# Two sweeps over each weight slab, and the gates' one-hot rows made one pair of slabs ahead, in a two-block transformer kernel on one core

## The chip, the cores and the metric

The kernel runs on one core of a Trainium2 chip. The core has five engines that are programmed apart and meet at semaphores: TensorE (PE, with its weight loads as PEld), VectorE (DVE), ScalarE (ACT), GpSimd (POOL) and SyncE (SP, which here issues DMAs). The metric is the device time of one execution, in microseconds (us), as the median of several runs; lower is better.

## The reference, cut to what matters

Two transformer blocks over 256 tokens of width 1024, batch 1, all in float32. The first has differential attention and stick-breaking attention side by side, cross attention to a memory of 256 tokens, and an MLP with a squared ReLU. The second has latent attention (MLA) and an RWKV7 recurrence side by side, and then a PEER layer that chooses 16 of 16384 experts for each of 8 heads of each token:

```python
def first_block(...):
    u = rms_norm(h, g_mix[l]) @ w_in[l]
    ...
    h = h + y @ w_out[l]
    h = h + cross_attention(rms_norm(h, g_cross[l]), rms_norm(mem, g_mem[l]), w_xq[l], w_xkv[l], w_xo[l])
    a = jnp.square(jax.nn.relu(rms_norm(h, g_mlp[l]) @ w_up[l]))
    h = h + a @ w_down[l]

def second_block(...):
    p = h @ w_in[l]
    y_a = mla_group(p[..., :MLA_COLS], ...)
    y_b = rwkv7_group(p[..., MLA_COLS:], ...)
    x = x + jnp.concatenate([y_a, y_b], axis=-1) @ w_o[l]
    x = x + peer_ffn(rms_norm_2(x, g_ffn[l]), w_pq[l], sub_keys[l], expert_u[l], expert_v[l])

def peer_ffn(...):            # inside, for 128 tokens at a time
    ...                       # top 16 of 128 keys twice, then top 16 of the 256 sums
    gate = jax.nn.softmax(top_s, axis=-1).astype(hb.dtype)
    act = jax.nn.gelu(jnp.einsum('thkd,td->thk', expert_u[idx], hb), approximate=False)
    return jnp.einsum('thk,thkd->td', gate * act, expert_v[idx])
```

## The kernel before

**Products in three parts.** A float32 product is made from three products of a narrower type. Each weight matrix comes in slabs of 128 x 1024 values (512 KB, one DMA on SP's queue, three buffers `raw`). `split` makes the slab's high part `hi` on ACT (line 329, three buffers) and then its low part `lo = raw - hi` on DVE (line 331, two buffers). The activations have such a pair too (`xsh`/`xsl`, `hbh`/`hbl` and others). For each 128-row piece of a slab `mm3` issues three products of 256 columns, one behind the other: hi by high activations (line 338), hi by low (line 339), lo by high (line 340). So the third product of a slab's very first piece already needs `lo`, and every later piece stands behind it, since PE works in the order of its instructions. In the MLP (`wide`) the first two are one product of 512 columns (line 398), and the third is at line 400. `lin_tok` and `Lin2.finish` have loops of their own (lines 476 to 478, and `mm3`).

**Stages.** In the profiled execution they are, roughly: first block's input and attentions up to 60 us, the rest of the first block up to 430, the second block's input, MLA and RWKV up to 700, the PEER layer's expert keys (`eu`, 128 slabs in 64 pairs, `u_pair`) up to 1110, and its values (`ev`, 128 slabs, lines 1774 to 1778) to the end. All 16384 experts are computed densely. Beside the `eu` pairs, DVE first works through `choose()` (the top-16 search), which ends with the halving sums of line 1655; after it come 32 gate groups of 8 tokens (`g_group`). A group makes one-hot rows `hot` and `wt` on DVE, multiplies them on PE (16 small products of line 1696) and puts the gates into `GA`. `GA` holds them next to the GELU of the keys' products.

**The order of the work.** The kernel is written against a scheduler that places the instructions of each engine's queue by their readiness in a simulated timeline and by their priority, which follows the order of the code unless `tc.high_priority` raises it. On the chip each engine then runs its queue in that order and waits at semaphores. So a change in one loop moves instructions that it doesn't name. The one on which this bears most is the RWKV part: a small triangular solve, in two rounds (`p_4977` is the first round's buffer, `p_4991` the second's), of short DVE instructions (lines 1152 to 1167), interleaved on DVE with MLA's key norm (`kg`, line 1370) for PE's scores (line 1375).

Of the kernel before, what the change touches and what calls it, by code (L numbers as in the profile page):

```python
# [20 lines left out]
P = 128  # L21
T = 256
D = 1024
KC = D // P
# [26 lines left out]
HI_BUFS = 3  # L51
LO_BUFS = 2
U_STEPS = 3
ATT_BUFS = 2
LIN_PS = 4
AHEAD_A = 2
# [158 lines left out]
def body(tc, A, out):  # L215
# [3 lines left out]
    with es:  # L219
# [117 lines left out]
        def mm3(ps, lh, ll, rh, rl, start, stop):  # L337
            PE.matmul(ps, lhsT=lh, rhs=rh, start=start, stop=False, skip_group_check=True)  # L338
            PE.matmul(ps, lhsT=lh, rhs=rl, start=False, stop=False, skip_group_check=True)  # L339
            PE.matmul(ps, lhsT=ll, rhs=rh, start=False, stop=stop, skip_group_check=True)  # L340

        def act_split(dst, src, j, scale=None):

            hi, lo = dst
            if scale is None:
                S.activation(hi[:, j], src, AF.Copy)
                V.tensor_tensor(lo[:, j], src, hi.bitcast(F32)[:, j], op=OP.subtract)
            else:
                S.activation(hi[:, j], src, AF.Identity, scale=scale)
                V.scalar_tensor_tensor(lo[:, j], src, scale, hi.bitcast(F32)[:, j], op0=OP.mult, op1=OP.subtract)  # L350
# [36 lines left out]
        def lin_part(ps, x, w, k, nb, c0, c1, first=True, wide=False):  # L387


            if ahead:  # L390
                w_ = ahead.pop(0)
                wh, wl = w_ if isinstance(w_, tuple) else split(w_)
            else:
                wh, wl = slab(w[nb][:, c0 * P:c1 * P], (c1 - c0) * P)
            for c in range(c0, c1):
                o = (c - c0) * P
                if wide:
                    PE.matmul(ps.rearrange("p (a t) -> p a t", a=2), lhsT=wh[:, o:o + P], rhs=x.both[:, c], start=first and c == 0,  # L398
                              stop=False, skip_group_check=True)
                    PE.matmul(ps[:, :T], lhsT=wl[:, o:o + P], rhs=x[0][:, c], start=False, stop=c == k - 1, skip_group_check=True)  # L400
                    continue
                mm3(ps[:, :T], wh[:, o:o + P], wl[:, o:o + P], x[0][:, c], x[1][:, c], first and c == 0, c == k - 1)

        def lin_T(x, w, k, nbs, evac, wide=None):

# [1271 lines left out]
            yield  # L1677


        def g_group(g, done):  # L1680

            hot = gp.tile([P, 2, 8, P], F16, tag="o1", name=nm("hot"), bufs=2)
            wt = gp.tile([P, 8, P], F16, tag="oh", name=nm("wt"), bufs=2)
            rows = lambda a: a.rearrange("p s t (a b) -> p (s t) a b", b=2)
            each = lambda a: a[:, g].rearrange("p s t b -> p (s t) b")[:, :, None].to_broadcast([P, 16, P // 2, 2])
            V.tensor_tensor(rows(hot), io[:, None].rearrange("p m (a b) -> p m a b", b=2).to_broadcast([P, 16, P // 2, 2]),
                            each(pk), op=OP.is_equal)
            parts = (wt, hot[:, 1])
            for s, dst in enumerate(parts):
                V.tensor_tensor(dst.rearrange("p t (a b) -> p t a b", b=2), hot[:, 1].rearrange("p t (a b) -> p t a b", b=2),  # L1690
                                pg[:, g, s, :, None].to_broadcast([P, 8, P // 2, 2]), op=OP.mult)
            ps = [pw(i) for i in range(2)]
            for i in range(8):
                p_, o_ = ps[i // 4], (i % 4) * P
                for s in range(2):
                    PE.matmul(p_[:, o_:o_ + P], lhsT=hot[:, 0, i], rhs=parts[s][:, i], start=i % 4 == 0 and s == 0,  # L1696
                              stop=i % 4 == 3 and s == 1, skip_group_check=True)
            for j in range(2):
                q = slice(8 * g + 4 * j, 8 * g + 4 * j + 4)
                p_ = ps[j].rearrange("p (t i) -> p i t", t=4)  # L1700
                if done:
                    V.scalar_tensor_tensor(GA[:, 0:done, q], p_[:, 0:done], 1 / GS, GA[:, 0:done, q], op0=OP.mult, op1=OP.mult)
                if done < P:
                    S.activation(GA[:, done:, q], p_[:, done:], AF.Copy, scale=1 / GS)

        def u_pair(c, td):

            ps = plin()
            for i in range(2):
                wh, wl = slab(A["eu"][c + i])  # L1710
                for k in range(KC):
                    ks = slice(k * P, k * P + P)
                    mm3(ps[:, i * T:i * T + T], wh[:, ks], wl[:, ks], hb[0][:, k], hb[1][:, k], i == 0 and k == 0,
                        i == 1 and k == KC - 1)
            pv_ = ps.rearrange("p (c t) -> p c t", c=2)
            dst = GA[:, c:c + 2]
            if td < T:
# [6 lines left out]

        steps = choose()
        next(steps)
        ng, first = 0, None
        for c in range(0, P, 2):
            u_pair(c, 8 * ng)
            if first is None:  # L1730
                for _ in range(U_STEPS):
                    if next(steps, mix) is mix:
                        first = c + 2
                        break
            else:
                want = min(32, ((c - first) // 2 + 1) * 32 // ((P - first - U_LAST) // 2))
                while ng < want:
                    g_group(ng, c + 2)
                    ng += 1

        acc = [[pw() for _ in range(2)] for _ in range(2)]
        res_ = [[x0("res", "h", 2 * t + d, F32).rearrange("p a t -> p (a t)") for d in range(2)] for t in range(2)]
# [55 lines left out]
```

## Time and profile before

| What | us |
|---|---|
| median of 3 runs | 1473.48 |
| lowest and highest of them | 1471.85, 1476.6 |
| the profiled execution | 1472.92 |
| its span in the trace | 1471.1 |

The profile is that of the one execution of 1472.92 us. Its trace spans 1471.1 us; the other 1.8 us lie around it. An engine's busy time counts its records, and a PE record is longer than the time PE takes until the next one starts, because matmuls overlap; so for PE the distance between starts says more than the busy share. A wait is printed in square brackets behind the instruction that waited, with the work that released it.

### The profile page before, as it was taken

How to read it: one execution, taken by the hardware profiler on the slowest of the kernel's cores; microseconds unless marked ns; L12 is line 12 of the kernel's file. 1: busy time of each engine (PE TensorE's matmuls, PEld its weight loads, DVE VectorE, ACT ScalarE, POOL GpSimd, SP SyncE). 2: the span in 40 equal slices, each digit the busy share in tenths (PEclk: the TensorE clock that was granted, in tenths of full speed). 3: DMA queues.
4: the chain of work that ended last, by engine and by line, in shares of the span. 5: the costliest groups of instructions: out<-in, count | busy, mean ns of one | idle time of the engine just before them, and what ended most of it. 6: DMA issues, size and time to landing. Idle time of an engine off the chain costs nothing.

```text
span 1471.1 us, 25614 instructions
## 1 busy us (share of the span) xinstructions
PE 1436.3 (98%) x9950; PEld 1296.2 (88%) x9950; DVE 1065.2 (72%) x1901; ACT 768.3 (52%) x1248; POOL 147.6 (10%) x159
## 2 busy tenths in 40 slices
PE   8999999999999979999999999999999999999998
PEld 7888999888888857799999999999998888888887
DVE  7876686886669997588998668788885555555554
ACT  7856655555556445463445454444445445444443
POOL 7400101000215352120000000000000000000000
PEclk9999999999999988999999999999999999999999
DMA  7553445666665411155555555555555655656664
GB/s 221 170 154 118 129 145 150 194 187 189 192 191 158 136 30 38 26 180 161 157 174 170 174 172 159 159 159 163 157 166 179 195 193 194 193 194 193 194 194 149
DMA packets 75914, 237.43 MB, mean 161 GB/s; under 512 B 14608, under 2 KB 17808, under 8 KB 75792
## 3 DMA queue, kind: packets, MB, share of 16 engines
q1 hardware_dynamic: 75792, 235.79, 52.2%
q8 instruction: 78, 1.28, 0.4%
q14 instruction: 44, 0.36, 0.1%
HBM read 233.27 MB, written 2.49 MB: 160 GB/s over the span
## 4 chain that ended last, share of the span: by engine, by line
PE 84%; DVE 9%; DMA 3%; ACT 1%; issue 1%; POOL 0%; SPq 0%; DVEq 0%; ACTq 0%
PE lin L340 13%; PE lin L338 13%; PE lin L339 12%; PE w L1774 8%; PE w L1775 8%; PE w L1778 8%; PE lin L398 7%; PE lin L400 3%; DVE lo L331 3%; PE w L1696 2%; DMA raw<-w_down 1%; DMA raw<-eu 1%; PE lin L476 1%; PE lin L478 1%; PE lin L477 1%
## 5 line engine op out<-in xcount | busy, mean ns | idle before, releaser
L331 DVE TENSOR_TENSOR lo<-raw,hi 128x1024 fp32r<-128x1024 f32 (+1 forms) x432 | 529.7, 1226 | 291.7 <-PE w L1775 92.7
L329 ACT ACTIVATE hi<-raw 128x1024 fp32r<-128x1024 f32 x437 | 458.6, 1050 | 464.7 <-PE lin L339 173.9
L340 PE MATMUL lin<-hbh,lo 128*128 128x256 f32 x1024 | 291.4, 287 | 4.1 <-DVE lo L331 4.1
L338 PE MATMUL lin<-hbh,hi 128*128 128x256 f32 x1024 | 291.7, 286 | 0.0
L339 PE MATMUL lin<-hbl,hi 128*128 128x256 f32 x1024 | 288.6, 283 | 0.0
L340 PEld LDWEIGHTS lin<-hbh,lo 128*128 128x128 f32 x1024 | 195.1, 191 | 6.3 <-DVE lo L331 6.0
L338 PEld LDWEIGHTS lin<-hbh,hi 128*128 128x128 f32 x1024 | 196.2, 192 | 0.3 <-ACT hi L329 0.2
L339 PEld LDWEIGHTS lin<-hbl,hi 128*128 128x128 f32 x1024 | 196.1, 192 | 0.0
L1775 PE MATMUL w<-lo,wh 128*128 128x512 f32 x504 | 155.3, 389 | 0.0
L1778 PE MATMUL w<-hi,wl 128*128 128x512 f32 x504 | 155.1, 389 | 0.0
L1774 PE MATMUL w<-hi,wh 128*128 128x512 f32 x504 | 134.8, 389 | 0.0
L1778 PEld LDWEIGHTS w<-hi,wl 128*128 128x128 f32 x504 | 94.6, 188 | 19.6
L1774 PEld LDWEIGHTS w<-hi,wh 128*128 128x128 f32 x504 | 94.5, 188 | 19.6
L1775 PEld LDWEIGHTS w<-lo,wh 128*128 128x128 f32 x504 | 94.5, 188 | 19.6
L398 PE MATMUL lin<-xs,hi 128*128 128x512 f32 x256 | 90.3, 398 | 0.3 <-ACT hi L329 0.3
L398 PE MATMUL lin<-a,hi 128*128 128x512 f32 x256 | 89.6, 394 | 0.0
L1757 ACT ACTIVATE wh<-GA 128x512 fp32r<-128x512 f32 x64 | 40.5, 634 | 74.0 <-PE w L1775 74.0
L400 PE MATMUL lin<-a,lo 128*128 128x256 f32 x256 | 71.4, 283 | 0.6 <-DVE lo L331 0.6
L400 PE MATMUL lin<-xs,lo 128*128 128x256 f32 x256 | 71.5, 281 | 0.0
L522 POOL TENSOR_TENSOR sqa<-sqa,sq 128x256 f32<-128x256 f32 x37 | 33.6, 909 | 315.0 <-ACT sq L518 301.3
L398 PEld LDWEIGHTS lin<-xs,hi 128*128 128x128 f32 x256 | 47.9, 188 | 12.1 <-ACT hi L329 0.7
L398 PEld LDWEIGHTS lin<-a,hi 128*128 128x128 f32 x256 | 47.6, 188 | 10.3
(566 smaller groups left out, 2868.8 us busy)
## 6 DMA issues: line engine op xcount, KB each, us to landing
raw<-eu SPq DMA_DIRECT2D x128, 512.0 KB, 3.6
raw<-ev SPq DMA_DIRECT2D x128, 512.0 KB, 3.5
raw<-w_up SPq DMA_DIRECT2D x32, 512.0 KB, 3.6
raw<-w_down SPq DMA_DIRECT2D x32, 512.0 KB, 4.7
raw<-w_in SPq DMA_DIRECT2D x20, 512.0 KB, 3.8
raw<-w_in_s SPq DMA_DIRECT2D x16, 512.0 KB, 3.6
raw<-w_pq SPq DMA_DIRECT2D x16, 512.0 KB, 3.7
raw<-w_in_m SPq DMA_DIRECT2D x8, 512.0 KB, 3.6
```

Source lines behind the costliest of these rows:

```text
L329: S.activation(hi[:, :n], raw[:, :n], AF.Copy)
L331: eng.tensor_tensor(lo[:, :n], raw[:, :n], hi.bitcast(F32)[:, :n], op=OP.subtract)
L338: PE.matmul(ps, lhsT=lh, rhs=rh, start=start, stop=False, skip_group_check=True)
L339: PE.matmul(ps, lhsT=lh, rhs=rl, start=False, stop=False, skip_group_check=True)
L340: PE.matmul(ps, lhsT=ll, rhs=rh, start=False, stop=stop, skip_group_check=True)
L398: PE.matmul(ps.rearrange("p (a t) -> p a t", a=2), lhsT=wh[:, o:o + P], rhs=x.both[:, c], start=first and c == 0, stop=False, skip_group_c ...
L400: PE.matmul(ps[:, :T], lhsT=wl[:, o:o + P], rhs=x[0][:, c], start=False, stop=c == k - 1, skip_group_check=True)
L522: G.tensor_tensor(self.acc, self.acc, q, op=OP.add)
L1757: S.activation(wh_, w2, AF.Copy)
L1774: PE.matmul(acc[t][d], lhsT=wh_[:, i, ts], rhs=vh[:, ds], start=c + i == 0, stop=False, skip_group_check=True)
L1775: PE.matmul(acc[t][d], lhsT=wh_[:, i, ts], rhs=vl[:, ds], start=False, stop=False, skip_group_check=True)
L1778: PE.matmul(acc[t][d], lhsT=wl_[:, i, ts], rhs=vh[:, ds], start=False, stop=False, skip_group_check=True)
```

## The change

A new function `sweeps3` takes the place of the loops in `lin_part` (the narrow and the wide form) and in `u_pair`. It goes over a slab twice: first all products with `wh` (16 of 256 columns, or 8 of 512), then the 8 products with `wl`. The number of products, their operands and the sums they go into are the same, their order within a slab is not. `Lin2.finish` and `lin_tok` stay as they are.

`g_group` is cut in two. `g_rows` makes a group's one-hot rows on DVE, one `u_pair` earlier than before in the code; `g_group` has the 16 products and the evacuation, and its products now have a raised priority (`GATE_PRIO`). `done`, the number of expert columns that a group finds complete, is larger by two for each group, which shifts the border between its DVE and its ACT part by two columns. The last two lines show that all 32 groups are made.

```diff
--- before.py
+++ after.py
@@ -51,6 +51,7 @@
 HI_BUFS = 3
 LO_BUFS = 2
 U_STEPS = 3
+GATE_PRIO = 300
 ATT_BUFS = 2
 LIN_PS = 4
 AHEAD_A = 2
@@ -339,6 +340,19 @@
             PE.matmul(ps, lhsT=lh, rhs=rl, start=False, stop=False, skip_group_check=True)
             PE.matmul(ps, lhsT=ll, rhs=rh, start=False, stop=stop, skip_group_check=True)
 
+        def sweeps3(ps, ks, wh, wl, x, start, stop, wide=False):
+
+            for c, o in ks:
+                at = start and c == ks[0][0]
+                if wide:
+                    PE.matmul(ps.rearrange("p (a t) -> p a t", a=2), lhsT=wh[:, o], rhs=x.both[:, c], start=at, stop=False,
+                              skip_group_check=True)
+                else:
+                    PE.matmul(ps[:, :T], lhsT=wh[:, o], rhs=x[0][:, c], start=at, stop=False, skip_group_check=True)
+                    PE.matmul(ps[:, :T], lhsT=wh[:, o], rhs=x[1][:, c], start=False, stop=False, skip_group_check=True)
+            for c, o in ks:
+                PE.matmul(ps[:, :T], lhsT=wl[:, o], rhs=x[0][:, c], start=False, stop=stop and c == ks[-1][0], skip_group_check=True)
+
         def act_split(dst, src, j, scale=None):
 
             hi, lo = dst
@@ -392,14 +406,8 @@
                 wh, wl = w_ if isinstance(w_, tuple) else split(w_)
             else:
                 wh, wl = slab(w[nb][:, c0 * P:c1 * P], (c1 - c0) * P)
-            for c in range(c0, c1):
-                o = (c - c0) * P
-                if wide:
-                    PE.matmul(ps.rearrange("p (a t) -> p a t", a=2), lhsT=wh[:, o:o + P], rhs=x.both[:, c], start=first and c == 0,
-                              stop=False, skip_group_check=True)
-                    PE.matmul(ps[:, :T], lhsT=wl[:, o:o + P], rhs=x[0][:, c], start=False, stop=c == k - 1, skip_group_check=True)
-                    continue
-                mm3(ps[:, :T], wh[:, o:o + P], wl[:, o:o + P], x[0][:, c], x[1][:, c], first and c == 0, c == k - 1)
+            ks = [(c, slice((c - c0) * P, (c - c0) * P + P)) for c in range(c0, c1)]
+            sweeps3(ps, ks, wh, wl, x, first and c0 == 0, c1 == k, wide)
 
         def lin_T(x, w, k, nbs, evac, wide=None):
 
@@ -1677,7 +1685,7 @@
             yield
 
 
-        def g_group(g, done):
+        def g_rows(g):
 
             hot = gp.tile([P, 2, 8, P], F16, tag="o1", name=nm("hot"), bufs=2)
             wt = gp.tile([P, 8, P], F16, tag="oh", name=nm("wt"), bufs=2)
@@ -1689,12 +1697,17 @@
             for s, dst in enumerate(parts):
                 V.tensor_tensor(dst.rearrange("p t (a b) -> p t a b", b=2), hot[:, 1].rearrange("p t (a b) -> p t a b", b=2),
                                 pg[:, g, s, :, None].to_broadcast([P, 8, P // 2, 2]), op=OP.mult)
+            return g, hot[:, 0], parts
+
+        def g_group(g, first, parts, done):
+
             ps = [pw(i) for i in range(2)]
-            for i in range(8):
-                p_, o_ = ps[i // 4], (i % 4) * P
-                for s in range(2):
-                    PE.matmul(p_[:, o_:o_ + P], lhsT=hot[:, 0, i], rhs=parts[s][:, i], start=i % 4 == 0 and s == 0,
-                              stop=i % 4 == 3 and s == 1, skip_group_check=True)
+            with tc.high_priority(offset=GATE_PRIO):
+                for i in range(8):
+                    p_, o_ = ps[i // 4], (i % 4) * P
+                    for s in range(2):
+                        PE.matmul(p_[:, o_:o_ + P], lhsT=first[:, i], rhs=parts[s][:, i], start=i % 4 == 0 and s == 0,
+                                  stop=i % 4 == 3 and s == 1, skip_group_check=True)
             for j in range(2):
                 q = slice(8 * g + 4 * j, 8 * g + 4 * j + 4)
                 p_ = ps[j].rearrange("p (t i) -> p i t", t=4)
@@ -1708,10 +1721,7 @@
             ps = plin()
             for i in range(2):
                 wh, wl = slab(A["eu"][c + i])
-                for k in range(KC):
-                    ks = slice(k * P, k * P + P)
-                    mm3(ps[:, i * T:i * T + T], wh[:, ks], wl[:, ks], hb[0][:, k], hb[1][:, k], i == 0 and k == 0,
-                        i == 1 and k == KC - 1)
+                sweeps3(ps[:, i * T:i * T + T], [(k, slice(k * P, k * P + P)) for k in range(KC)], wh, wl, hb, i == 0, i == 1)
             pv_ = ps.rearrange("p (c t) -> p c t", c=2)
             dst = GA[:, c:c + 2]
             if td < T:
@@ -1724,7 +1734,8 @@
 
         steps = choose()
         next(steps)
-        ng, first = 0, None
+
+        ng, first, rows_ = 0, None, []
         for c in range(0, P, 2):
             u_pair(c, 8 * ng)
             if first is None:
@@ -1734,9 +1745,11 @@
                         break
             else:
                 want = min(32, ((c - first) // 2 + 1) * 32 // ((P - first - U_LAST) // 2))
-                while ng < want:
-                    g_group(ng, c + 2)
-                    ng += 1
+                for made in rows_:
+                    g_group(*made, c + 2)
+                ng += len(rows_)
+                rows_ = [g_rows(g) for g in range(ng, max(ng, want))]
+        assert ng == 32 and not rows_
 
         acc = [[pw() for _ in range(2)] for _ in range(2)]
         res_ = [[x0("res", "h", 2 * t + d, F32).rearrange("p a t -> p (a t)") for d in range(2)] for t in range(2)]
```

Three places where the queues differ follow, and a fourth in counts. The first is PE's queue at the first slab behind the attention's key products (`lin_638` is the sum's bank, `hi_641` and `lo_643` the slab's parts, `xsh_` and `xsl_` the activations' parts). Before:

```order
L338 MATMUL lin_638<-xsh_131,hi_641 128x256
L339 MATMUL lin_638<-xsl_135,hi_641 128x256
L340 MATMUL lin_638<-xsh_131,lo_643 128x256
...
L338 MATMUL lin_638<-xsh_132,hi_641 128x256
L339 MATMUL lin_638<-xsl_136,hi_641 128x256
L340 MATMUL lin_638<-xsh_132,lo_643 128x256
```

Each piece of the slab brings its product with `lo_643` third. After the change (lines 351 and 352 are the narrow products with `wh`, 354 that with `wl`):

```order
L351 MATMUL lin_638<-xsh_131,hi_641 128x256
L352 MATMUL lin_638<-xsl_135,hi_641 128x256
...
L351 MATMUL lin_638<-xsh_134,hi_641 128x256
L352 MATMUL lin_638<-xsl_138,hi_641 128x256
L354 MATMUL lin_638<-xsh_131,lo_643 128x256 x2
L354 MATMUL lin_638<-xsh_132,lo_643 128x256 x2
L354 MATMUL lin_638<-xsh_133,lo_643 128x256 x2
L354 MATMUL lin_638<-xsh_134,lo_643 128x256 x2
```

The first product with `lo_643` stood third and now stands seventeenth. On DVE that split stands in the same place in both, with the same work ahead of it and behind it.

The second is DVE's queue at the end of `choose()`, beside the `eu` slabs. `GA` and `pg` here are the search's working tiles, `lo_` the slabs' low parts (one number is the same slab in both). Before:

```order
L1646 TENSOR_TENSOR GA<-ab,io 128x4096
L331 TENSOR_TENSOR lo_8979<-raw_8975,hi_8977 128x1024
L1651 TENSOR_TENSOR GA<-GA,n_7822 128x4096
L331 TENSOR_TENSOR lo_9026<-raw_9022,hi_9024 128x1024
L1676 SCALAR_TENSOR_TENSOR pg<-w_9399,pg 128x32x16
L1655 TENSOR_TENSOR GA<-GA 128x256x8
L331 TENSOR_TENSOR lo_9056<-raw_9052,hi_9054 128x1024
L1655 TENSOR_TENSOR GA<-GA 128x256x4
L331 TENSOR_TENSOR lo_9101<-raw_9097,hi_9099 128x1024
L1655 TENSOR_TENSOR GA<-GA 128x256x2
```

Before, one split stands between most steps of the search. After the change the same steps stand among later slabs' splits:

```order
L1654 TENSOR_TENSOR GA<-ab,io 128x4096
L332 TENSOR_TENSOR lo_9056<-raw_9052,hi_9054 128x1024
L332 TENSOR_TENSOR lo_9101<-raw_9097,hi_9099 128x1024
L1659 TENSOR_TENSOR GA<-GA,n_7822 128x4096
L1684 SCALAR_TENSOR_TENSOR pg<-w_9399,pg 128x32x16
L332 TENSOR_TENSOR lo_9131<-raw_9127,hi_9129 128x1024
L1663 TENSOR_TENSOR GA<-GA 128x256x8
L332 TENSOR_TENSOR lo_9178<-raw_9174,hi_9176 128x1024
L1663 TENSOR_TENSOR GA<-GA 128x256x4
L332 TENSOR_TENSOR lo_9208<-raw_9204,hi_9206 128x1024
L1663 TENSOR_TENSOR GA<-GA 128x256x2
```

The last halving sum (`GA 128x256x2`, line 1655 before and 1663 after) follows the split `lo_9101` before and `lo_9208` after: three slabs later.

The third is DVE's queue in the RWKV solve, from the first round's reduction to its last copy. Before:

```order
L1161 TENSOR_REDUCE t_1019_5896<-p_4977 64x64
L1438 TENSOR_TENSOR ksq_5953<-lin_6229,rk_4890 64x512
L1370 TENSOR_TENSOR kg_6105<-kgu_5954,n_1055_6097 128x512
L1131 TENSOR_TENSOR AB_5957<-w_5970,cst 128x2x256
L1164 TENSOR_TENSOR p_4977<-p_4977,t_1019_5896 64x512
L1131 TENSOR_TENSOR AB_5957<-w_5971,cst 128x2x256
L1378 MEMSET lin_6269 64x2x64
L1166 TENSOR_REDUCE p_4977<-p_4977 64x8x8
L1382 TENSOR_REDUCE msm_6273<-lin_6269 128x1
L1131 TENSOR_TENSOR AB_5957<-w_6054,cst 128x2x256
L1167 COPY p_4977<-p_4977 64x256
```

The copy of line 1167 ends the round, and all of it stands ahead of the second round. After the change the end of the first round's solve reads (line 1175 is line 1167 of before, 1378 is 1370):

```order
L1172 TENSOR_TENSOR p_4977<-p_4977,t_1019_5896 64x512
L1169 TENSOR_REDUCE t_1059_6123<-p_4991 64x32
L1399 TENSOR_SCALAR me_6330<-me_6330,msm_6329 128x128
L1174 TENSOR_REDUCE p_4977<-p_4977 64x8x8
L501 SCALAR_TENSOR_TENSOR n_1085_6291<-n_1086_6292,n_1085_6291 128x512
L1172 TENSOR_TENSOR p_4991<-p_4991,t_1059_6123 64x64 x2
L1175 COPY p_4977<-p_4977 64x256
L1378 TENSOR_TENSOR kg_6299<-kgu_5954,n_1085_6291 128x512
```

Before, the first round's copy ends 8 rows after the key norm `kg_6105` and ahead of the second round's start. After, it is mixed with the second round's rows (`p_4991`), and stands 42 rows behind `kg_6105`; the next key norm, `kg_6299`, follows it at once.

The fourth is the small products of the gate groups on PE. Before they stand in 69 runs of 2 to 16 (line 1696) with slab products between, after in 37 runs (line 1709), of which 26 hold a whole group of 16.

## Rows read from the trace of the kernel before

**Rows 1.** The page: the span, the engines' busy time, and the chain that ended last

```profile
span 1471.1 us, 25614 instructions
...
PE 1436.3 (98%) x9950; PEld 1296.2 (88%) x9950; DVE 1065.2 (72%) x1901; ACT 768.3 (52%) x1248; POOL 147.6 (10%) x159
...
PE 84%; DVE 9%; DMA 3%; ACT 1%; issue 1%; POOL 0%; SPq 0%; DVEq 0%; ACTq 0%
```

**Rows 2.** Table of stretches: length, five engines' busy, clock, DMA share, GB/s

```profile
40.00:60.00 20.00, 17.84 (x113) 16.16 (x112) 14.85 (x29) 17.20 (x40) 11.74 (x13) 0.91 0.54 177
430.00:500.00 70.00, 67.59 (x502) 62.06 (x500) 63.69 (x99) 42.17 (x69) 33.46 (x39) 0.98 0.48 149
500.00:575.00 75.00, 63.67 (x472) 52.29 (x469) 67.58 (x156) 36.76 (x77) 28.89 (x21) 0.90 0.23 56
...
700.00:810.00 110.00, 105.86 (x864) 103.85 (x864) 104.77 (x365) 50.13 (x59) 0.24 (x1) 1.00 0.56 165
820.00:1108.00 288.00, 287.95 (x2638) 284.84 (x2637) 218.60 (x285) 137.33 (x238) 0.00 (x0) 1.00 0.54 163
```

**Rows 3.** Waits of PE, PEld in six stretches to 820 us: total, times, longest

```profile
PEld lin L340 <- DVE lo L331: 0.5, 2, 0.4
...
PE lin L340 <- DVE lo L331: 2.2, 1, 2.2
...
PE lin L400 <- DVE lo L331: 0.6, 2, 0.3
...
PE lin L340 <- DVE lo L331: 1.8, 1, 1.8
...
PE lin L1375 <- DVE kg L1370: 4.1, 1, 4.1
...
PE lin L340 <- DVE lo L331: 4.1, 8, 1.1
```

**Rows 4.** Timeline of PE at a gate group's end: start, length, operation

```profile
901.87 0.22 PE L1696 MATMUL w<-wt,hot 128*128 128x128 f16 x1
901.93 0.22 PE L1696 MATMUL w<-hot 128*128 128x128 f16 x1
901.96 0.36 PE L338 MATMUL lin<-hbh,hi 128*128 128x256 f32 x1
902.16 0.28 PE L339 MATMUL lin<-hbl,hi 128*128 128x256 f32 x1
902.28 0.28 PE L340 MATMUL lin<-hbh,lo 128*128 128x256 f32 x1
```

**Rows 5.** Timeline of PE at one of the eight last waits, in square brackets

```profile
793.26 0.39 PE L340 MATMUL lin<-hbh,lo 128*128 128x256 f32 x1 [0.52 <-DVE lo L331]
793.48 0.28 PE L338 MATMUL lin<-hbh,hi 128*128 128x256 f32 x1
```

**Rows 6.** Timeline of PE from 45 to 55 us

```profile
45.34 0.28 PE L338 MATMUL lin<-xsh,hi 128*128 128x256 f32 x1
...
47.89 0.38 PE L340 MATMUL lin<-xsh,lo 128*128 128x256 f32 x1 [2.16 <-DVE lo L331]
...
48.36 0.42 PE L340 MATMUL lin<-xsh,lo 128*128 128x256 f32 x1
48.57 0.42 PE L338 MATMUL lin<-xsh,hi 128*128 128x256 f32 x1
...
55.00 0.27 PE L720 MATMUL w<-ident,w 128*128 128x128 f32 x1
```

**Rows 7.** Timeline of DVE beside it

```profile
46.62 1.21 DVE L331 TENSOR_TENSOR lo<-raw,hi 128x1024 fp32r<-128x1024 f32 x1
47.76 2.57 DVE L350 SCALAR_TENSOR_TENSOR ms<-qk,pv,ms 128x256 fp32r<-128x256 f32 x4
50.45 1.55 DVE L331 TENSOR_TENSOR lo<-raw,hi 128x1024 fp32r<-128x1024 f32 x1
```

**Rows 8.** Timeline of DVE in the RWKV solve

```profile
541.00 0.87 DVE L1167 COPY p<-p 64x256 f32<-64x256 f32 x1
...
553.65 0.68 DVE L1370 TENSOR_TENSOR kg<-kgu,n 128x512 f32<-128x512 f32 x1
...
560.48 0.69 DVE L1204 TENSOR_TENSOR p<-w,cst 128x512 f32<-128x512 f32 x1
```

## The prediction

> **What bounds the kernel now.** I read the page first: PE has records over 98% of the span and holds 84% of the chain that ended last, DVE 9% [rows 1]. So PE bounds it, and a change that alters no product can only win back time in which PE stands still or runs slowly. The table of stretches shows where that is [rows 2]. From 820 to 1108 us PE has records over 287.95 of 288 us and the clock is full: there is nothing to win but the small joints between kinds of products. From 700 to 810 PE lacks 4.1 us of 110 while DVE is busy for 104.77. From 430 to 575 PE lacks 13.7 us of 145, DVE is busy for 91% and then 90%, and the clock falls to 0.98 and 0.90. The list of waits then says what was late there [rows 3]: line 340, the third product of a slab's first piece, waits for DVE's low part `lo` two times before 40 us (0.5 us, at the weight load), once at 45 us (2.2), twice in the wide form (0.6), once near 485 us (1.8) and eight times from 700 to 820 (4.1). The longest other wait is line 1375 for MLA's key norm, 4.1 us.
>
> **What a wait costs.** A narrow product is followed by the next 0.12 us later, though its record lasts 0.28 (starts at 902.16 and 902.28) [rows 4]. So the first 0.16 us of a delay lie inside the record ahead and are not printed. And behind a wait the next start is 0.22 us away, not 0.12 [rows 5], 0.10 lost once more. A wait printed as w thus costs about w + 0.26.
>
> **The change part by part.** All terms are against the profiled execution, 1472.92 us; it lies 0.56 below the median of the runs, so the two can be used alike.
>
> The sweeps neither add nor remove products. A slab's first low product moves from third to seventeenth place, 14 products x 0.12 = 1.7 us later, so `lo` may come 1.7 us later before PE waits. In the wide form it moves from second to ninth among fewer, longer products. The buffers of `lo` come free at the slab's last product, as before; those of `hi` come free earlier, which only helps ACT. No DMA is moved past another on SP's queue, and POOL's count is the same.
>
> Before 40 us: the 0.5 us of the weight load go, all being under 1.7. Gain 0.5.
>
> At 45 us I lay the products out anew [rows 6, 7]. Sixteen high ones from 45.34 end at 47.26; `lo` lands at 46.62 + 1.21 = 47.83, with the same work ahead of it on DVE in both queues, so PE still waits 0.6 instead of 2.16, and the eight low ones end at 47.89 + 0.10 + 0.96 = 48.95. The next slab's high ones end at 50.87. Its `lo` stands behind four instructions on DVE and lands at 50.45 + 1.55 = 52.00: a new wait of 1.1 us. The low ones end near 53.1, where before PE was done with both slabs at 55.00. Gain 1.9; with starts 0.21 apart, as they were at half level after the wait (48.36, 48.57), the new wait soaks most of that up and the gain is 1.7. I take 1.8.
>
> The wide form: 0.6 + 2 x 0.26 = 1.1, all of it covered by the longer lead.
>
> Near 485 us: 1.8 + 0.26, and the clock with it. 70 us at 0.98 is 1.4 us lost [rows 2], so 3.5 is the most. DVE's 63.69 of 70 us leave little room: a wait may come back one slab later, so the lower end is 0. I take half, 1.8.
>
> From 500 to 575 us the solve and MLA are reordered on DVE without a change of their own. The key norm stands earlier in the queue, and PE's wait of 4.1 for it shrinks or goes. The first round's last copy moves from its place at 541.00 to just ahead of the next key norm, which was at 553.65: 12.7 us later [rows 8]. Its first use on DVE by way of PE is line 1204 at 560.48, so 18.6 us lay between; the 12.7 eat slack and cost nothing as long as the copies out and back and the products in between fit in the 5.9 left. The nearest bounds: the whole wait with its clock loss on one side (4.1 and about half as much again, +6), the same amount less slack on the other (-4). I take +1.0.
>
> From 700 to 820 us: eight waits, 4.1 + 8 x 0.26 = 6.2, each at most 1.1 us and so below the new lead of 1.7. Against it stands that DVE is busy for 95% of that stretch: what it cannot do in time it will be late with again. But the search's last step now stands three slabs later. Three slabs are 3 x 24 x 0.12 = 8.6 us of PE, and DVE has three more splits to make in them, 3 x 1.21 = 3.6 [rows 7]; 5.0 us of DVE's work have moved out of the tight stretch into one where it is busy for 218.60 of 288. So 5.0 to 6.2 can be had. I take 5.5. The search's end comes later and with it the gates; the groups stand behind on DVE and ACT, off PE's path, and their last evacuation still lies four slabs ahead of the `ev` stage, 4 x 2.88 = 11.5 us of cover. If that cover went, each slab of it would cost up to 2.88.
>
> The gate groups: a run's last small product is followed after 0.03 us instead of 0.06, then the slab's first product takes 0.20 instead of 0.12 [rows 4]: about 0.05 us a run. There are 37 runs instead of 69, so 32 x 0.05 = 1.6. The one-hot rows are the same DVE instructions, a pair of slabs earlier, and make PE's raised products ready when they come up; a group that waited would hold the whole of PE's queue, but DVE is at 76% there, and I cost it at nothing.
> On this the Trainium skill speaks otherwise (TensorE: Matmul & The Clock Gate, "Step-by-step: what each phase is for"): the engine pulls the next weight load ahead of the products in flight, so a switch of operands should be covered. By that rule the term would be 0 and the forecast 1.6 us higher; the row with 0.20 speaks for a small price.
>
> Sum: 0.5 + 1.8 + 1.1 + 1.8 + 1.0 + 5.5 + 1.6 = 13.3 us, so 1472.9 - 13.3 = 1459.6, rounded to **1460 us**.
>
> **The rivals.** *More* (1453 us): the key norm's wait goes with its clock loss (+6.0 instead of +1.0) and the stretch near 485 us gives all its 3.5. That is 6.7 more than the forecast. For it speaks that the norm stands earlier in DVE's queue, 42 rows ahead of the round's last copy where it stood 8; against it, that DVE is busy for 90% there and something else will be late.
>
> *DVE is the bound where the waits are* (1468 us): from 430 to 575 and from 700 to 810 us DVE's work is a fixed amount that PE's slabs follow, so a wait taken away at one slab returns at a later one. Then the terms 1.8, 1.0 and 5.5 go, and 0.5 + 1.8 + 1.1 + 1.6 = 5.0 are left: 1467.9. For it: 95% and 91% busy [rows 2]; against it: the 5.0 us of DVE's work that leave the stretch.
> The Trainium skill would expect this one (Perfetto Trace Analysis, "Identifying the Most-Contended Engine"): the engine with the highest occupancy is to be made faster first, and it counts DVE's occupancy as a fair measure. Here PE's own records are near as dense there, so the rows don't decide.
>
> *Slower* (about 1481 us): the first round of the solve ends 12.7 us later and what uses it had no slack after all. PE has nothing to fill that with; and from 500 to 575 us it stood without records for 11.3 us while the clock of 0.90 lost 7.5 of 75, 0.66 us for each us idle. So 12.7 x 1.66 = 21 us lost, less the other terms' 12.3: 8.8 slower. It decides from a delay of about 10 us beyond the slack; before, 18.6 us lay between, which speaks against it.
>
> *No change* (1473 us): the scheduler's other moves give back what the sweeps win, in stretches that I counted at nothing. Against it stands that PE has no other waits of size outside the stretches named.
>
> **How the numbers follow.** The forecast 0.60, more 0.12, DVE-bound 0.18, slower 0.06, no change 0.04. The range reaches from the rival with more, 1453 less a microsecond for the rounding of its terms, to the DVE-bound one with as much: 1452 to 1469, which leaves out 0.10. About 0.3%, 4.4 us, is what a measurement of this kernel can tell from no change. The forecast and *more* are faster by over that (0.72), and of the DVE-bound rival, which lies 5.0 below, a little under half (0.08): 0.80 faster. The rest of it with no change gives 0.14 same, and 0.06 slower.
>
> **What would show it.** In the trace after, waits of the low product (now line 354) for `lo` should be near 1.7 us in all before 60 us, in two places, and none from 700 to 820 us, with PE over 109 of 110 us there. DVE's stretch from 820 on should be fuller. PE's records from 500 to 575 us should come to 64 to 68 us of the same work. If low products still wait eight times after 700 us, the rival on DVE is right; if PE stands idle at lines 1204 to 1225 (1212 to 1233 after), the solve's delay had no slack. The prediction is wrong above all if the reorder of the solve moves more than 6 us either way.

## The result

The changed kernel takes 1457.21 us as the median of four runs (1454.77 to 1457.8), where the kernel before took 1472.76 beside it. The ratio is 0.9893, with a 95% interval of 0.9875 to 0.9912: 15.6 us faster, 13 to 18. Forecast were 1460 us and 1452 to 1469. The profiled execution took 1457.07 us.

The page of the kernel after, as [rows 1]: the span, the busy time of the engines, and the chain that ended last.

```profile
span 1455.3 us, 25592 instructions
...
PE 1421.4 (98%) x9950; PEld 1287.5 (88%) x9950; DVE 1061.5 (73%) x1900; ACT 767.3 (53%) x1248; POOL 148.1 (10%) x159
...
PE 90%; DVE 6%; DMA 2%; ACT 1%; issue 1%; SPq 0%; POOL 0%; DVEq 0%; ACTq 0%
```

PE has as many records as before. Its share of the chain has grown from 84 to 90%, and DVE's has fallen from 9 to 6: PE waits less for DVE. The table of stretches of after, in the columns of [rows 2] (by now the same clock time is not quite the same work):

```profile
40.00:60.00 20.00, 18.67 (x123) 16.04 (x122) 16.32 (x31) 16.16 (x38) 13.78 (x13) 1.00 0.57 184
430.00:500.00 70.00, 65.10 (x496) 60.49 (x494) 63.55 (x97) 40.78 (x67) 34.42 (x39) 1.00 0.46 143
500.00:575.00 75.00, 63.03 (x471) 50.98 (x471) 66.15 (x161) 37.42 (x79) 28.74 (x21) 0.89 0.21 55
575.00:660.00 85.00, 83.18 (x824) 74.55 (x823) 57.64 (x122) 48.77 (x103) 18.57 (x14) 1.00 0.34 105
700.00:810.00 110.00, 109.28 (x908) 108.80 (x908) 103.58 (x347) 54.33 (x62) 0.00 (x0) 1.00 0.55 178
820.00:1108.00 288.00, 288.00 (x2632) 285.02 (x2631) 224.58 (x292) 136.97 (x240) 0.00 (x0) 1.00 0.53 163
```

From 700 to 810 us PE now has records over 109.28 us and not 105.86, and 908 products instead of 864, while DVE is nearly as full as before (103.58 us and 104.77). Behind 820 us DVE is fuller, with 224.58 us instead of 218.60, as the prediction had it. From 500 to 575 nothing is better. The longest waits of PE, by stretch (one before 40 us, one from 40 to 60, two from 430 to 500, one from 500 to 575, one from 700 to 820 us):

```profile
PE lin L351 <- DVE qk L635: 1.9, 1, 1.9
...
PE lin L351 <- ACT hi L330: 1.3, 1, 1.3
...
PE lin L351 <- DVE pr L1014: 1.7, 1, 1.7
...
PE lin L354 <- DVE lo L332: 1.4, 2, 0.9
...
PE lin L1405 <- DVE me L1399: 6.5, 1, 6.5
...
PE lin L354 <- DVE lo L332: 0.7, 1, 0.7
```

PE waits for `lo` four times in the whole span and not twelve, and for 0.7 instead of 4.1 us after 700 us. Other waits stand in the first places of the early stretches: for sum banks that DVE empties (`qk`, `pr`), for `hi`, and one of 6.5 us for MLA's softmax weights `me`.

To see where the gain came from I took PE's time between the starts of its products, less the usual distance for a product of its kind (the median in the kernel before, 0.12 us for a narrow one), and summed it over stretches that hold the same amount of work (the same sum of usual distances) in both traces. That is PE's lost time, waits, hidden parts and half clock together:

| Work that stood before at (us) | lost before | lost after | won | forecast |
|---|---|---|---|---|
| 0 to 33 | 1.9 | 4.8 | -2.9 | 0.5 |
| 33 to 55 | 3.5 | 1.2 | 2.2 | 1.8 |
| 55 to 250 | 5.0 | 5.5 | -0.5 | 0 |
| 250 to 425 (the MLP) | 0.7 | -1.7 | 2.4 | 1.1 |
| 425 to 500 | 6.2 | 4.6 | 1.7 | 1.8 |
| 500 to 575 | 25.4 | 27.4 | -2.0 | 1.0 |
| 575 to 700 | 12.7 | 4.8 | 7.9 | 0 |
| 700 to 820 | 7.3 | 1.6 | 5.7 | 5.5 |
| 820 to 1115 | 4.3 | 2.1 | 2.2 | 1.6 |

Each number is rounded by itself. The parts add up to 16.6; the rest of the work is 0.1 longer, and the span ends 5.6 us behind the start of the last product where it ended 5.0 behind it, which leaves, to a tenth, the spans' 15.8.

### The profile page after: what moved, and what is told of

Read it like the earlier page. It is cut to its first block, busy times and chain, and to the rows that moved or that the text cites. A ratio compares the mean times of both kernels' runs of the same rounds, so it can differ in the third digit from the quotient of the medians.

```text
span 1455.3 us, 25592 instructions
## 1 busy us (share of the span) xinstructions
PE 1421.4 (98%) x9950; PEld 1287.5 (88%) x9950; DVE 1061.5 (73%) x1900; ACT 767.3 (53%) x1248; POOL 148.1 (10%) x159
## 4 chain that ended last, share of the span: by engine, by line
PE 90%; DVE 6%; DMA 2%; ACT 1%; issue 1%; SPq 0%; POOL 0%; DVEq 0%; ACTq 0%
PE lin L354 17%; PE lin L351 13%; PE lin L352 13%; PE lin L348 8%; PE w L1788 8%; PE w L1787 8%; PE w L1791 8%; PE w L1709 2%; DVE lo L332 1%; PE lin L484 1%; PE lin L485 1%; PE lin L486 1%; DMA raw<-w_pq 1%; PE w L1623 0%; PE lin L513 0%
## 5 line engine op out<-in xcount | busy, mean ns | idle before, releaser
L351 PE MATMUL lin<-hbh,hi 128*128 128x256 f32 x1024 | 253.0, 284 | 0.0
L352 PE MATMUL lin<-hbl,hi 128*128 128x256 f32 x1024 | 252.3, 284 | 0.0
L354 PE MATMUL lin<-hbh,lo 128*128 128x256 f32 x1024 | 145.0, 284 | 0.7 <-DVE lo L332 0.7
L354 PEld LDWEIGHTS lin<-hbh,lo 128*128 128x128 f32 x1024 | 132.1, 192 | 1.1 <-DVE lo L332 1.1
L348 PE MATMUL lin<-a,hi 128*128 128x512 f32 x256 | 64.8, 395 | 0.0
L348 PE MATMUL lin<-xs,hi 128*128 128x512 f32 x256 | 63.3, 392 | 0.0
L354 PE MATMUL lin<-xs,lo 128*128 128x256 f32 x384 | 53.8, 285 | 0.0
L354 PEld LDWEIGHTS lin<-xs,lo 128*128 128x128 f32 x384 | 50.9, 191 | 2.2
```

The lines of the kernel that those rows point to most:

```text
L351: PE.matmul(ps[:, :T], lhsT=wh[:, o], rhs=x[0][:, c], start=at, stop=False, skip_group_check=True)
L352: PE.matmul(ps[:, :T], lhsT=wh[:, o], rhs=x[1][:, c], start=False, stop=False, skip_group_check=True)
L354: PE.matmul(ps[:, :T], lhsT=wl[:, o], rhs=x[0][:, c], start=False, stop=stop and c == ks[-1][0], skip_group_check=True)
```

## The experiments

The first theory is the **lead**: what counts is that a slab's low part may come 1.7 us later. Its rivals are **DVE's throughput** (waits only move), **the groups** (the gates' rows and priority carry the gain), and **order** (what the scheduler moves elsewhere does it).

**The sweeps without the new gates, and the new gates without the sweeps.** The first has the kernel before with `sweeps3` in `lin_part` and `u_pair`; the second has `g_rows`, the later `g_group` and its priority, with the old loops.

> The sweeps in lin_part and u_pair alone; the gate groups as before the change. If the lead of the low part is the cause, the gain is the whole one less the gate groups' share: PE's time between 818 and 1112 us lost 5.4 us before and 2.1 after, so 2 to 3.4 us less than the 15.6 gained: 1459 to 1461 us. PE waits for the low part at most in two or three places before 700 us and nowhere from 700 to 820. If the gates' rows and their priority carried it, no more than half would be left, 1465 or above.

> The gates' rows a pair ahead and the raised priority alone; all slabs in the old order. By the price of a run's end (0.05 us, 32 runs fewer) 1.6 us faster, up to 3.4 by the trace after: 1469 to 1471 us. The eight waits for the low part from 700 to 820 us (4.1 us) stay. If the groups were the larger cause: under 1465.

```profile
PE lin L353 <- DVE lo L331: 0.7, 1, 0.7
```

```profile
PE lin L341 <- DVE lo L332: 4.2, 8, 1.1
```

Measured: 1457.55 us for the sweeps alone, ratio 0.9905 (0.9887 to 0.9922), 14 us won; 1470.82 us for the gates alone, ratio 0.9987 (0.9975 to 0.9999), 2 us won, and the eight waits stay (the lines are PE's waits from 692 to 820 us, of the first kernel and of the second). What is won is worked out from the ratio, here and for the sweeps by stage; the medians lie further apart, 15.7 and 2.4 us. So the groups' theory falls. The trace tells more: the sweeps alone have the groups' products in 32 runs, fewer than the full change with its 37, and the gates alone have 47 where there were 69. After 820 us the sweeps alone lose 1.7 us, the full change 2.1, the gates alone 2.6 and the kernel before 4.3 (the 5.4 of the expectation was too high, since it didn't hold both traces to the same work). So either half of the change takes joints away, the sweeps take more without the priority than with it, and beside the sweeps the new gates win nothing that the runs show.

**The sweeps by stage.** One kernel has them in `u_pair` alone, one in `lin_part` alone.

> The sweeps in u_pair alone, gate groups as before. Lead: the eight waits of 700 to 820 us go with what is hidden about them, 5 to 6 us: 1467 us, and nothing is changed before 700 us. DVE-bound rival: the waits come back at later slabs and under 2 us are won, 1471 or above.

> The sweeps in lin_part alone. The eight waits from 700 to 820 us stay at about 4 us; what is won lies before 700 us. By the trace after that part gave 6 us by 700 us (a loss of 2.8 before 33 us, 2.1 won at 45, 4 in the MLP, and 5.6 from 500 to 700): 1466 to 1468 us. If only the waits for the low part mattered, 0.5 + 1.8 + 1.1 + 1.8 = 5.2 and no more: 1468. The gains of e3 and e4 should add up to that of e1 within 2 us, if the stages are independent.

Measured: 1464.02 us, ratio 0.9953 (0.9935 to 0.9971), 6.9 us; and 1465.22 us, ratio 0.9956 (0.9942 to 0.9969), 6.5 us. They add up to 13.4, and both at once gave 14 (by the medians 9.2 and 8.0, and 15.7). The first table row below is of `u_pair` alone, from 700 to 810 us, in the columns as above; the waits are those of PE from 692 to 820 us, of `u_pair` alone and of `lin_part` alone.

```profile
700.00:810.00 110.00, 109.37 (x914) 109.17 (x913) 105.78 (x358) 54.10 (x62) 0.24 (x1) 1.00 0.57 175
...
PE lin L353 <- DVE lo L331: 0.6, 1, 0.6
```

```profile
PE lin L340 <- DVE lo L331: 5.9, 9, 1.0
```

With sweeps PE is full there and DVE nearly so. Without, after a first part that hands over earlier, PE waits nine times and 5.9 us, more than the 4.1 of before.

**The second block's slabs alone.** `lin_part` sweeps from 430 us on; the rest is as before.

```diff
+        late = []                      # filled behind the MLP's last product
 def lin_part(...):
...
+    if late:
...
+        sweeps3(ps, ks, wh, wl, x, first and c0 == 0, c1 == k, wide)
+        return
     for c in range(c0, c1): ...
```

> The sweeps in lin_part from the second block on alone (from 430 us); first block, u_pair and gate groups as before. The stretches before 430 us should be those of before, with the 2.2 us wait at 45 us. If the 7.6 us that the changed kernel lost less from 575 to 700 us (and the 2 more from 500 to 575) come from the second block's slabs themselves, 5 to 7 us are won: 1466 to 1468 us. If they come from what the first block hands on, under 2 us are won: 1471 or above.

Measured: 1472.23 us, ratio 0.9992 (0.9975 to 1.0009), which is no difference by its timed runs; its profiled execution is 3.4 us shorter than that of before. In that trace the work from 575 to 700 us lost 4.9 us and not 12.7, as in the full change, and that from 500 to 575 lost 2.4 more. But the work from 700 to 820 us lost 9.7 instead of 7.3. So the gain is made by the second block's own slabs, and about a third of it is given back at once where the expert slabs are still in the old order:

```profile
PE lin L341 <- DVE lo L332: 6.0, 9, 1.1
```

The first expectation did not hold. The number of the second came, under 2 us, but not for its reason: the gain of that stretch is there in the trace, and it does come from the second block. What a stage before 700 us wins is not all kept unless `u_pair` has the lead too. The timed runs can't settle how much.

**Half the lead.** `u_pair` sweeps over four pieces at a time, so that the first low product is ninth and not seventeenth.

```diff
-                sweeps3(ps[:, i * T:i * T + T], [(k, ...) for k in range(KC)], wh, wl, hb, i == 0, i == 1)
+                for h in range(0, KC, 4):
+                    sweeps3(ps[:, i * T:i * T + T], [(k, ...) for k in range(h, h + 4)], wh, wl, hb,
+                            i == 0 and h == 0, i == 1 and h == 4)
```

> The changed kernel, u_pair in half sweeps: the high products of four pieces, their low ones, then the other four. The first low product stands ninth instead of seventeenth, so it is 0.72 us later than in the old order and not 1.68. If the lead decides, of the eight old waits (0.2 to 1.1 us, 0.16 more each as hidden) those of 0.7 and 1.1 us come back in part: two to four waits, together 0.5 to 1.5 us, from 700 to 820 us, and 1458 to 1459 us. If any order with a little lead does, there is no difference; if DVE is the bound, 3 us or more of waits.

```profile
PE lin L354 <- DVE lo L332: 3.2, 5, 1.0
```

Measured: five waits and 3.2 us from 692 to 820 us, and 1459.08 us, ratio 0.9906 (0.9875 to 0.9937). The size of the lead decides: the stretch loses 5.3 us with half of it, 1.6 with all of it and 7.3 with none. The waits are more than the lead's theory gave, 0.5 to 1.5 us, and as many as the expectation had named for DVE as the bound, 3 us or more. DVE falls behind by more than the old waits show, so throughput has a part.

**More work for DVE.** In both kernels a quarter of the low part is made twice for the first 40 expert slabs.

```diff
-                wh, wl = slab(A["eu"][c + i])
+                raw_ = load(A["eu"][c + i])
+                wh, wl = split(raw_)
+                if c < 40:
+                    V.tensor_tensor(wl[:, :256], raw_[:, :256], wh.bitcast(F32)[:, :256], op=OP.subtract)
```

> The changed kernel with more work on DVE: for each of the first 40 eu slabs a quarter of the low part is made a second time (128x256, some 0.35 us each by its own share of the 1.22 us split, 14 us in all), and PE needs it. If a slab's lead of 1.7 us is what counts, DVE may fall behind by that and the search may end later: under 3 us lost against the changed kernel. If DVE is the bound from 700 to 820 us (busy for 103.6 of 110, so 6.4 to spare), 14 - 6.4 = 7 us or more are lost.

> The same addition in the kernel before. With the old order PE has no lead to give: each slab's split is 0.35 us later for PE's third product, so the waits of 4.1 us in 8 places from 700 to 820 us grow to many more: 7 to 14 us lost against the kernel before, 1480 to 1487 us. If both kernels lose the same, DVE's throughput and not the lead sets the time.

```profile
PE lin L354 <- DVE lo L1726: 16.5, 14, 2.2
```

```profile
PE lin L340 <- DVE lo L1713: 24.1, 9, 5.1
```

Measured: 1478.45 us for the changed kernel with it (1455.79 without, in the same rounds) and 1507.38 for the kernel before (1473.3 without). The addition is 40 operations of 0.42 us, 17 us. It cost 22.7 us in the one and 34.1 in the other; the lines are PE's waits for `lo`, of the changed kernel and of the kernel before. The first is what was expected if DVE is the bound (7 us or more), and of the second 7 to 14 was expected. So DVE's throughput does bind in this stretch once DVE gets a little more to do, against what I expected of the lead, and the lead still saves 11 us (8 by the ratios, 1.0043 and 1.0224, against 0.9875 and 1). The rival's mechanism is real; the changed kernel stands just on the good side of it, with DVE busy for 103.58 of 110 us.

**No priority for the groups' products.** `GATE_PRIO` is 0 instead of 300; the rows are still made ahead.

> The changed kernel without the raised priority of the groups' small products (offset 0). The rows are still made a pair ahead. If the number of runs sets the groups' price (0.05 to 0.06 us a run), the loss follows the runs that its queue shows: as many as in the kernel before would cost 1.8 us, 1459; if the rows made ahead are what matters, nothing changes.

Measured: 1470.23 us, ratio 0.9977 (0.9959 to 0.9995): 13 us of the gain are gone, and neither expectation was near. Its queue has the groups' 512 products in 238 runs, of which 199 are one small product between two of a slab. The timeline of PE, start and length:

```profile
959.67 0.36 PE L351 MATMUL lin<-hbh,hi 128*128 128x256 f32 x1
959.87 0.23 PE L1709 MATMUL w<-wt,hot 128*128 128x128 f16 x1
959.91 0.36 PE L352 MATMUL lin<-hbl,hi 128*128 128x256 f32 x1
960.12 0.23 PE L1709 MATMUL w<-hot 128*128 128x128 f16 x1
```

A slab product and a small one take 0.24 us together (959.67 to 959.91), where they take 0.12 + 0.06 apart: 0.066 us for each run by the unrounded distances. Times 238 - 37 runs that is 13.3 us, the whole loss; the trace has it in the work after 820 us, which takes 14.0 us longer than in the changed kernel. Rows made ahead can run at any time, and without the priority the scheduler strews their products over the slabs. In these kernels the priority is needed only because the rows are made ahead: the sweeps alone have neither, and 32 runs.

**One split held back.** The 1.9 us at 24 us are a wait for a sum bank. The timeline of PE and of DVE there, in the changed kernel:

```profile
25.83 0.36 PE L351 MATMUL lin<-xsh,hi 128*128 128x256 f32 x1 [1.93 <-DVE qk L635]
...
27.27 0.42 PE L352 MATMUL lin<-xsl,hi 128*128 128x256 f32 x1
27.48 0.42 PE L351 MATMUL lin<-xsh,hi 128*128 128x256 f32 x1
```

```profile
23.41 1.21 DVE L332 TENSOR_TENSOR lo<-raw,hi 128x1024 fp32r<-128x1024 f32 x1
24.55 0.81 DVE L576 TENSOR_SCALAR trig<-trig 128x256 f32<-128x256 f32 x1
25.27 1.07 DVE L635 TENSOR_TENSOR qk<-lin,rb 128x256 f32<-128x256 f32 x3
```

In the queue before, the split that starts here at 23.41 stood behind the three evacuations `qk`; now it stands ahead of them, PE gets its bank 2 us late, and the products from 27.27 on are 0.21 us apart, at half clock (1.2 GHz; the granted clock before 40 us is 0.96, and was 1.00). The experiment puts that one split back, and the rest of DVE's queue stays.

```diff
+            if len(seen) == 2 and len(hold) == 3:      # this one slab; hold: the evacuations qk
+                with tc.issue_after(hold[0].ins):
+                    eng.tensor_tensor(lo[:, :n], raw[:, :n], hi.bitcast(F32)[:, :n], op=OP.subtract)
...
```

> The changed kernel, with one split on DVE (lo_387, the fifth slab of the first input product) held behind the three evacuations that give PE its sum banks back, as it stands in the queue before the change. If the 1.9 us that PE waited at 24 us after the change, and the half clock from 27.1 to 30.5 behind it, come from that order alone, the wait goes and 2 to 3.5 us are won: 1454 to 1455 us. If PE was short there for another reason, the wait returns under another name and the time stays at 1457.

> The changed kernel as it is, on the same chip and in the same rounds as the next one, to compare the two: 1457 us.

> The changed kernel with the one split held, again, on the chip and in the rounds of the changed kernel: 2 to 2.5 us faster than it by the traces (lost time 54.1 against 56.5 us). If the traces' difference was chance, none.

```profile
PE lin L491 <- DVE t L638: 2.7, 1, 2.7
```

Measured: 1456.4 us, ratio 0.9887 (0.9861 to 0.9912) the first time; then, in one set of rounds, 1459.12 (0.9897, 0.9877 to 0.9916) with the split held and 1455.79 (0.9875, 0.9856 to 0.9895) for the changed kernel as it is. The wait for `qk` is gone in both, but a little later PE waits for `t`, the next evacuation, 1.0 us the first time and the 2.7 of the line above the second. Lost time on that work was 2.8 and 4.2 us, with the split where the change puts it 4.8 and 4.6. The wait returned under another name, as the second expectation had it, and nothing is won that can be measured. DVE is late in this stretch, and its order only says for whom. How late differs between two executions of one kernel: with the split held, DVE begins the evacuations at 22.17 us in the first and at 23.31 in the second.

## Why the prediction was right, point by point

**Right in the main term.** From 700 to 820 us 5.5 us were forecast and 5.7 came, and for the reason given: with sweeps in `u_pair` the waits go, with half sweeps most stay. The shift of the search is there too: its last halving sum ends at 806.06 us before (line 1655), while PE is at the 32nd key slab, and at 802.22 us after (line 1663), while PE is at the 36th.

```profile
805.40 0.66 DVE L1655 TENSOR_TENSOR GA<-GA 128x512 f16<-128x512 f16 x1
```

```profile
801.55 0.67 DVE L1663 TENSOR_TENSOR GA<-GA 128x512 f16<-128x512 f16 x1
```

The rival on DVE's throughput, at 0.18, was nearer than that number says: 40 more operations on DVE bring it out in full.

**Right at 45 us, by another wait.** 1.8 were forecast, 2.2 came. PE did not wait for the first slab's `lo` at all, since it came there 2.8 us late itself and `lo` only 2.3; the second slab waits 1.3 us, as forecast (1.1), but for `hi`, not for `lo`.

**Near in size, with wrong reasons: the joints and the MLP.** After 820 us 2.2 came instead of 1.6. It can be counted almost without the usual distances: from the first product of the 37th key slab to the 101st of the values' first line (1774, then 1787) PE took 367.89 us before and 366.76 after, with nine more products in between (1.1 us by their usual distances). Over 32 runs that is 0.07 us a run. The price in the forecast was 0.05, and the 14.0 us of the 201 runs more without the priority give 0.07 as well. The rule of the Trainium skill that I weighed against it (TensorE: Matmul & The Clock Gate, "Step-by-step: what each phase is for"), that the next weight load is pulled ahead, by which I took a switch to be covered, would have given 0; the run with 238 joints, at 0.24 us a pair, shows the price. I ascribed the fewer runs to the gates' priority; the sweeps alone bring 32.

In the MLP 2.4 came instead of 1.1. Beside the waits, the products of 512 columns keep a closer distance: 0.230 us where it was 0.233, by the medians of all 512 of them, some 1.5 us. That is not the work of the new order. Three kernels that keep a wide and a narrow product in turn in the MLP (the gates alone, `u_pair` alone, the second block alone) have 0.230 as well, and the first two lose 2.1 and 1.6 us less there than the kernel before. What sets this distance from kernel to kernel stays open, so a part of these 2.4 us is not shown to come from the sweeps.

**Wrong: before 40 us.** I read the orders of the queues at three places and took the rest as unchanged. At 24 us a split had moved ahead of three evacuations. Forecast 0.5 won, found 2.9 lost. The place was there to be read in the order, but the order alone does not cost that much: the sweeps alone, `lin_part` alone, half the lead, no priority and more work for DVE have the split ahead of the evacuations too; PE waits there for 0.5 to 1.4 us, the granted clock stays at 1.00, and 0.6 to 1.2 us are lost against the kernel before. The second profile of the changed kernel has the wait of 1.9 us and the fall of the clock again, with 2.6 lost. What makes DVE later in the changed kernel than in those five stays open.

**Wrong in its parts: the solve.** From 500 to 575 us -2.0 came, within the bounds of -4 to +6; the value taken, 1.0, had the wrong sign. The key norm's wait went, as said, and the first round's last copy came at 554.48 us, just ahead of the next key norm, as read from the order. In place of the old wait PE waits 6.5 us for `me`:

```profile
543.14 2.00 PE L1198 MATMUL w<-tk,AB 128*128 128x64 f32 x16 [1.33 <-DVE AB L1139]
551.60 0.90 PE L1405 MATMUL lin<-ident,me 128*128 128x128 f32 x3 [6.46 <-DVE me L1399]
```

DVE's timeline shows what it did ahead of `me`, which needs the reciprocal in the first line:

```profile
549.31 0.15 DVE L1394 RECIPROCAL msm<-msm 128x2 f32<-128x2 f32 x1
549.38 0.66 DVE L1169 TENSOR_REDUCE t<-p 64x64 f32<-64x512 f32 x1
549.97 1.38 DVE L1167 TENSOR_TENSOR p<-p 64x64 f32<-64x64 f32 x2
551.27 0.27 DVE L1399 TENSOR_SCALAR me<-me,msm 128x128 f32<-128x128 f32 x1
```

MLA's softmax stands behind the rounds of the solve, which run mixed on DVE. That is not the rival *slower*, whose sign was PE idle at lines 1212 to 1233: no wait of PE of 0.2 us or more stands there. The solve's delay had its slack. What came late was another step on DVE, which the prediction expected only in general ("something else will be late") and put no time to.

**Put at nothing without a reason: 575 to 700 us.** The largest error of the sum lies here: 0 was forecast and 7.9 came. The prediction says that PE has no other waits of size outside the stretches that it names. But the trace of before has two waits for `hi` here, 1.2 us (575 to 660 us) and 2.2 (660 to 700), and the clock falls in two stretches. The lines are those waits, the one for `hi` that is left after (0.8), and the two stretches before and after:

```profile
PE lin L338 <- ACT hi L329: 1.2, 1, 1.2
...
PE lin L338 <- ACT hi L329: 2.2, 1, 2.2
```

```profile
PE lin L351 <- ACT hi L330: 0.8, 1, 0.8
```

```profile
575.00:600.00 25.00, 25.00 (x206) 20.51 (x206) 16.41 (x42) 13.87 (x32) 5.10 (x4) 0.95 0.12 32
650.00:675.00 25.00, 22.42 (x171) 21.97 (x170) 20.40 (x48) 11.70 (x20) 0.00 (x0) 0.93 0.60 190
```

```profile
575.00:600.00 25.00, 25.00 (x201) 20.85 (x200) 16.46 (x40) 15.49 (x37) 6.46 (x4) 1.00 0.11 32
650.00:675.00 25.00, 23.40 (x194) 23.04 (x194) 24.25 (x69) 10.99 (x18) 0.00 (x0) 1.00 0.62 195
```

By these rows the clock cost 0.05 x 25 + 0.07 x 25 = 3.0 us before and nothing after. All eight kernels with sweeps in these slabs lose 4 to 5 us on that work and the four others 10 to 14, so the gain comes with the sweeps; whether through the lead of these slabs or through the solve's new order was not taken apart and stays open.

The range held because errors of -3.4 and -3.0 stood against errors of +7.9, +1.3 and +0.6. The direction was earned, the closeness of the sum was partly luck.

## What to carry to other kernels

Where a product needs a cheap operand and an expensive one, issue all products with the early operand first: the lead adds no work, and here this order, with 1.7 us of lead in each slab, won 14 us of 1473. It hides lateness, not a lack of throughput, so look at how full the engine behind it is, and give the lead to the stage behind too, or part of the gain of the stage ahead turns into its waits (here about a third). Where a scheduler decides, read the whole difference of the queues, also in stages that the change doesn't name, and keep small products together: work that can run at any time gets strewn.

## What was not expected of the hardware

A product of 256 columns (f32) and one of 128 (f16) in turn on PE take 0.24 us a pair, against 0.18 for the same two in rows of their own; 201 such joints more cost 13 us. Products of 512 and 256 columns, both f32, show no such price: in turn they took 0.347 to 0.353 us a pair in the MLP, in rows of their own 0.348 to 0.351. Whether the type or something else makes the difference, no run here shows. And an addition of 17 us of work on DVE, in a stretch where it was 94% busy, cost 23 us with the lead and 34 without, more than the work itself. PE's clock fell as well, to 0.95 and 0.84 in the stretch from 700 to 810 us of the two kernels; by an estimate from these rows, 0.05 x 110 = 5.5 and 0.16 x 110 = 17.6 us went that way, about what 23 and 34 have over 17:

```profile
700.00:810.00 110.00, 92.93 (x703) 89.06 (x702) 103.86 (x369) 43.79 (x50) 0.00 (x0) 0.95 0.46 139
```

```profile
700.00:810.00 110.00, 80.96 (x568) 78.27 (x567) 102.34 (x374) 34.30 (x41) 0.24 (x1) 0.84 0.34 104
```
